# Latent attention on one Trainium2 core: joining the two halves of a head's output by a vector add instead of a shift matmul

## The chip, the cores and the metric

The kernel runs on one core of a Trainium2 chip. The metric is the device time in microseconds of one execution, as the median of several runs. TensorE does the matmuls and the transposes into PSUM; VectorE, ScalarE and GpSimd do the element-wise work, and only the first two of these touch PSUM here; SyncE, ScalarE and GpSimd issue DMAs.

## What is computed

Two decoder layers over 1024 positions of width 1024. Each projects the residual stream once; the columns feed a gated linear recurrence (8 heads), a latent attention (8 heads) and an attention into 256 memory tokens (4 heads). Each group's output is gated, the groups are concatenated, projected back and normalised. The change touches the latent attention alone, whose core is

```
for l in range(DEPTH):
    ...
    y_mla = _mla_group(...)          # 8 heads, 64 value columns each
    ...
    y = concatenate([y_hg * silu(hg_gate), y_mla * silu(mla_gate), y_mem * silu(mem_gate)])
    x = layernorm(ALPHA * x + y @ w_out[l])

# inside _mla_group, per block of 128 queries
s = (einsum('bqhd,bkhd->bhqk', qn, k_nope) + einsum('bqhr,bkr->bhqk', qr, k_rope)) * scale
p = softmax(where(key_idx <= q_idx, s, NEG_BIG))
o = einsum('bhqk,bkhd->bqhd', p, v)
```

All data are f32. To keep the precision, the kernel writes each operand of a product as the sum of a rounded part and a remainder (`split`, L288) and forms the product from three matmuls (`mm3`, L262).

## The kernel before, in words

A layer runs through its stages one after another: memory attention, the latents, the recurrence, the latent attention (`mla_prep`, L913, and `mla_attend`, L965), the output product (`out_group`, L1155). The latent attention takes about 736 to 892 us in the first layer and 1806 to 1978 us in the second.

`mla_attend` walks over 32 steps: 8 heads `hd`, and for each four pairs `j` of query blocks, 256 queries. A pair of query blocks sees 2j + 2 blocks of 128 keys, so the pairs grow from j = 0 to j = 3. For a step:

- `scores` (L992) forms the score matrix of two query blocks in PSUM (tile `A`, two buffers), adds the causal mask by a matmul with the identity (L1014), takes the negated row maximum `nm` on VectorE (L1017), the exponential `pr` with its row sum `rs` on ScalarE (L1020), the reciprocal on VectorE (L1021) and the scaling on GpSimd (L1024). It is called one step ahead.
- `turn` (L1029) transposes the probabilities of a pair of key blocks on TensorE (L1034) and splits them into `ph` on ScalarE (L289) and the remainder `pl` on VectorE (L290).
- `values` (L1042) multiplies them with the values. The weight tile `VV` holds a head's 64 value columns twice: the rounded part in columns 0 to 63, the remainder in 64 to 127. So one matmul with `ph` (L1058) and one with `pl` (L1059) write a sum of 128 rows into a PSUM tile `B` of 256 columns, whose lower 64 rows (0 to 63) hold one half of the result and whose rows 64 to 127 hold the other. These units are queued, and one is taken when more than three wait.
- After the last unit of a step, ScalarE copies the 128 rows into `ol` (L1062). One unit later `close` (L1065) multiplies this copy by a constant matrix `shift` (L1069), which moves rows 64 to 127 onto rows 0 to 63 and adds them to the sum in PSUM. VectorE then multiplies rows 0 to 63 by the head's gate (L1072), and a DMA writes the result `yt` to `Yd` in DRAM (L1073).

An even head's result lies in partitions 0 to 63 of `yt`, an odd head's in 64 to 127 (`rw`). Between the steps come the query products of the next head (`q_proj`, L971, with L985 on ScalarE and L986 on VectorE), for every second head its keys (`k_proj`, `k_odd`, L943 and L956), and in the last head the first weight and input tiles of the output product (L1136, L1145). The source gives the order of the calls; a scheduler sets the order of the instructions on each engine, and each engine runs its queue in that order.

The matrix is made once at the start: GpSimd clears it (L157) and ScalarE copies 64 columns of the identity into it (L158).

Of the kernel before, what the change touches and what calls it, by code (L numbers as in the profile page):

```python
# [7 lines left out]
F32 = mybir.dt.float32  # L8
F32R = mybir.dt.float32r
# [3 lines left out]
ALU = mybir.AluOpType  # L13
# [4 lines left out]
P = 128  # L18
# [23 lines left out]
C_ID = 0  # L42
# [39 lines left out]
def program(tc, xT, xtok, memT, pos, w_in, small, w_uq, w_uk, w_uv, w_mk, w_mv,  # L82
            w_out, ln_g, ln_b, cst, msk, out):
    nc = tc.nc
    es = ExitStack()

    def pool(name, **kw):
        return tc.tile_pool(name=name, **kw)

    cp = es.enter_context(pool("cp", bufs=1))  # L90
# [26 lines left out]
    def T(pl, shape, dt=F32, tag=None, bufs=None):  # L117
        n_name[0] += 1
        return pl.tile(shape, dt, tag=tag, name=f"{tag}_{n_name[0]}", bufs=bufs)
# [7 lines left out]
    def f32(t):  # L127
        return t.bitcast(F32)
# [8 lines left out]
    NSM = small.shape[1]  # L137
    sm = T(cp, [P, NSM], F32, "sm")

    shift = T(cp, [P, P], F32R, "shift")  # L140
    mhalf = T(cp, [P, 8], F32, "mhalf")
    nc.gpsimd.memset(mhalf, -0.5)
    ones = T(cp, [P, 2], F32, "ones")
# [9 lines left out]
    def constants(lp):  # L153
        cs = T(wpc[1], [P, 2048], F32, "raw", 2)[:, 0:C_N]
        nc.scalar.dma_start(cs, cst)
        nc.scalar.dma_start(sm, small)
        nc.gpsimd.memset(f32(shift), 0.0)  # L157
        nc.scalar.copy(shift[:, 0:64], cs[:, C_ID + 64:C_ID + P])  # L158
        nc.scalar.copy(idr, cs[:, C_ID:C_ID + P])
        for i, c in enumerate((C_BE, C_BO)):  # L160
            nc.scalar.copy(bias_r[i], cs[:, c:c + P])
# [803 lines left out]
    def mla_attend(l, cqT, ckT, KK, uq, kv, k_proj, k_odd, rtab, VV, lp, rp):  # L965
        uqh, uql = (t.rearrange("p (r c) -> p r c", r=2) for t in uq)
        gs = []
# [72 lines left out]
        opss = {}  # L1040

        def values(hd, j, cp_, ph, pl_):  # L1042
            hp, ab = hd // 2, hd % 2
            rw = slice(64 * ab, 64 * ab + 64)
            if cp_ == 0:
                opss[hd, j] = psB()
            ops = opss[hd, j][:, 0:256].rearrange("p (b q) -> p b q", b=2)
# [10 lines left out]
                nc.tensor.matmul(ov, lhsT=w, rhs=rh, start=kb_ == 0, stop=False)  # L1058
                nc.tensor.matmul(ov, lhsT=w, rhs=rl, start=False, stop=kb_ == 2 * j + 1)  # L1059
            if cp_ == j:  # L1060
                t = T(lp, [P, 256], F32R, "ol", 1)
                nc.scalar.copy(t, opss[hd, j][:, 0:256])  # L1062
                return t

        def close(hd, j, t):  # L1065
            hp, ab = hd // 2, hd % 2
            rw = slice(64 * ab, 64 * ab + 64)
            ops = opss.pop((hd, j))
            nc.tensor.matmul(ops[:, 0:256], lhsT=shift, rhs=t, start=False, stop=True, skip_group_check=True)  # L1069
            s_ = slice(j * 256, (j + 1) * 256)  # L1070
            yt = T(lp, [P, 256], F32, "yt", 2)
            nc.vector.tensor_tensor(out=yt[rw], in0=ops[0:64, 0:256], in1=gs[hp][rw, s_], op=ALU.mult)  # L1072
            (nc.gpsimd if hd == 7 and j > 1 else nc.sync).dma_start(Y[8 + hp, rw, s_], yt[rw])  # L1073

        def v_proj(tb):
# [49 lines left out]
        if ends:  # L1125
            close(*ends.pop())
# [201 lines left out]
    for l in range(DEPTH):  # L1328
# [4 lines left out]
        ops = latents_out(l, X, tp)  # L1333
# [75 lines left out]
```

## Time and profile before

| | |
|---|---|
| median of 3 runs | 2161.31 us (2160.71 to 2161.49) |
| profiled execution, its own time | 2163.67 us |
| its span, from first to last instruction | 2161.9 us |
| mean granted TensorE clock | 0.986 |
| first and last shift matmul | 736.6 and 1977.8 us |

The views of the profile used here are these. The page's first part gives for each engine its busy time, the share of the span and the number of instructions. A table by windows gives the same for stretches of time, with the granted clock and the DMA load. A view by line gives the duration of a line's instructions, what its engine waited for before them and who waited for them. A time line lists single instructions: start, duration, engine, line, operation, tiles written and read, and in brackets the engine's idle time ahead of it with what ended it. The chain of waits goes back from the last instruction of the program, at each step to what released it. PE is TensorE's matmul, PEld its weight load, DVE VectorE, ACT ScalarE, POOL GpSimd, SP SyncE.

### The profile page before, as it was taken

How to read it: one execution, taken by the hardware profiler on the slowest of the kernel's cores; microseconds unless marked ns; L12 is line 12 of the kernel's file. 1: busy time of each engine (PE TensorE's matmuls, PEld its weight loads, DVE VectorE, ACT ScalarE, POOL GpSimd, SP SyncE). 2: the span in 40 equal slices, each digit the busy share in tenths (PEclk: the TensorE clock that was granted, in tenths of full speed). 3: DMA queues.
4: the chain of work that ended last, by engine and by line, in shares of the span. 5: the costliest groups of instructions: out<-in, count | busy, mean ns of one | idle time of the engine just before them, and what ended most of it. 6: DMA issues, size and time to landing. Idle time of an engine off the chain costs nothing. (4 is left out here: it accounts for less than half of the span.)

```text
span 2161.9 us, 30334 instructions
## 1 busy us (share of the span) xinstructions
PE 2065.4 (96%) x11176; PEld 1752.7 (81%) x11176; DVE 1459.8 (68%) x2665; ACT 1009.8 (47%) x1999; POOL 375.3 (17%) x516
## 2 busy tenths in 40 slices
PE   9997999999999899999899989999999997999998
PEld 7887888888887788788687878888888886888886
DVE  6536777777777788566764366777777776887524
ACT  5534343434343677444554444434443436775311
POOL 0212000000001445211111220000000014543112
PEclk9999999999999999999999989999999999999999
DMA  5413101111114301456761131111111134015322
GB/s 199 132 59 127 52 27 59 40 59 40 59 40 162 116 15 38 152 188 229 234 194 47 59 130 41 40 59 39 59 40 50 49 131 146 13 40 180 109 66 78
DMA packets 122100, 194.47 MB, mean 90 GB/s; under 512 B 8608, under 2 KB 90400, under 8 KB 121952
## 3 DMA queue, kind: packets, MB, share of 16 engines
q1 hardware_dynamic: 100560, 145.91, 20.8%
q10 hardware_dynamic: 13840, 22.24, 3.1%
q0 software_dynamic: 7552, 24.39, 3.0%
q8 instruction: 88, 1.44, 0.3%
q14 instruction: 60, 0.49, 0.1%
HBM read 151.09 MB, written 41.42 MB: 89 GB/s over the span
## 5 line engine op out<-in xcount | busy, mean ns | idle before, releaser
L263 PE MATMUL Y<-x,wh 128*128 128x512 f32 x576 | 233.9, 406 | 0.0
L265 PE MATMUL Y<-x,wl 128*128 128x512 f32 x576 | 232.4, 404 | 0.0
L264 PE MATMUL Y<-x,wh 128*128 128x512 f32 x576 | 228.3, 396 | 0.0
L249 DVE TENSOR_TENSOR wl<-raw,wh 128x512 fp32r<-128x512 f32 (+2 forms) x216 | 141.3, 701 | 102.0 <-ACT wh L248 81.9
L264 PE MATMUL Y<-t,wh 128*128 128x512 f32 x432 | 170.9, 396 | 0.0
L263 PE MATMUL Y<-t,wh 128*128 128x512 f32 x432 | 169.9, 393 | 0.0
L265 PE MATMUL Y<-t,wl 128*128 128x512 f32 x432 | 168.9, 391 | 0.0
L289 ACT CAST wh<-raw 128x512 fp32r<-128x512 f32 (+1 forms) x124 | 72.9, 592 | 199.8 <-DMA raw<-in_w_in 132.5
L248 ACT CAST wh<-raw 128x512 fp32r<-128x512 f32 (+2 forms) x216 | 118.7, 605 | 98.4 <-PE A L264 49.8
L289 ACT CAST wh<-S 128x512 fp32r<-128x512 f32 x144 | 89.5, 622 | 138.2 <-DVE S L687 61.6
L573 PEld LDWEIGHTS B<-Q,r 128*128 128x128 f32 x896 | 115.5, 191 | 38.8 <-issue 13.5
L1024 POOL TENSOR_SCALAR pr<-pr,rs 128x512 f32<-128x512 f32 (+1 forms) x192 | 116.8, 617 | 147.9 <-DVE rs L1021 132.6
L573 PE MATMUL B<-Q,r 128*128 128x128 f32 x896 | 132.2, 291 | 7.9 <-DVE Q L552 7.8
L290 DVE TENSOR_TENSOR pl<-B,ph 128x512 fp32r<-128x512 f32 (+1 forms) x192 | 119.9, 644 | 22.4 <-ACT ph L289 19.0
L290 DVE TENSOR_TENSOR wl<-raw,wh 128x512 fp32r<-128x512 f32 (+1 forms) x124 | 80.8, 655 | 80.2 <-ACT wh L289 79.8
L265 PEld LDWEIGHTS Y<-x,wl 128*128 128x128 f32 x576 | 109.2, 190 | 20.4
L263 PEld LDWEIGHTS Y<-x,wh 128*128 128x128 f32 x576 | 109.6, 190 | 19.2
L264 PEld LDWEIGHTS Y<-x,wh 128*128 128x128 f32 x576 | 109.3, 190 | 19.4
L1020 ACT ACTIVATE pr<-A,nm 128x128 f32<-128x128 f32 (+7 forms) x128 | 95.5, 747 | 57.8 <-DVE nm L1017 54.3
L289 ACT CAST ph<-B 128x512 fp32r<-128x512 f32 (+1 forms) x192 | 102.7, 554 | 36.3 <-PE B L1034 20.4
L285 POOL TENSOR_TENSOR rst<-ss,mhalf 128x4 f32<-128x4 f32 x32 | 36.4, 1137 | 474.1 <-DVE ss L283 455.7
L263 PE MATMUL A<-wh,yh 128*128 128x512 f32 x288 | 112.7, 396 | 5.6 <-ACT wh L248 3.6
(337 smaller groups left out, 5583.6 us busy)
## 6 DMA issues: line engine op xcount, KB each, us to landing
raw<-in_w_in SPq DMA_DIRECT2D x84, 512.0 KB, 4.6
raw<-in_w_out SPq DMA_DIRECT2D x32, 1024.0 KB, 5.4
yr<-Yd SPq DMA_DIRECT2D x28, 384.0 KB, 4.8
Yd<-r POOLq DMA_DIRECT2D x32, 256.0 KB, 2.6
raw<-in_w_mk SPq DMA_DIRECT2D x8, 512.0 KB, 4.8
raw<-in_w_mv SPq DMA_DIRECT2D x8, 512.0 KB, 4.4
t<-in_xT SPq DMA_DIRECT2D x16, 256.0 KB, 3.2
Yd<-yt POOLq DMA_DIRECT2D x16, 256.0 KB, 2.3
```

The lines of the kernel that those rows point to most:

```text
L248: nc.scalar.copy(h[:, s_], raw[:, s_])
L249: nc.vector.tensor_tensor(out=lo[:, s_], in0=raw[:, s_], in1=f32(h[:, s_]), op=ALU.subtract)
L263: nc.tensor.matmul(o, lhsT=lh, rhs=rh, start=first, stop=False, **kw)
L264: nc.tensor.matmul(o, lhsT=lh, rhs=rl, start=False, stop=False, **kw)
L265: nc.tensor.matmul(o, lhsT=ll, rhs=rh, start=False, stop=last, **kw)
L285: nc.gpsimd.tensor_tensor(out=r[:, 0:k], in0=ss, in1=mhalf[:, 0:k], op=ALU.pow)
L289: nc.scalar.copy(h, src)
L290: nc.vector.tensor_tensor(out=lo, in0=src, in1=f32(h), op=ALU.subtract)
L573: nc.tensor.matmul(lp[:, pr * P:(pr + 1) * P], lhsT=xp[:, pr * P:(pr + 1) * P], rhs=q_moving(Q, pr, b), start=True, stop=True)
L1020: nc.scalar.activation(po, sv, AF.Exp, bias=nm, scale=1.0, accum_out=rs)
L1024: nc.gpsimd.tensor_scalar(out=pr[:, c0:c1], in0=pr[:, c0:c1], scalar1=rs, scalar2=0.0, op0=ALU.mult, op1=ALU.add)
```

## The change

The shift matrix and the shift matmul go. ScalarE copies only rows 64 to 127 of the sum, now as plain f32 into one of two buffers; VectorE adds this copy to rows 0 to 63 and writes `yt`, and a second vector instruction multiplies `yt` by the gate in place.

```diff
-    shift = T(cp, [P, P], F32R, "shift")
...
-        nc.gpsimd.memset(f32(shift), 0.0)
-        nc.scalar.copy(shift[:, 0:64], cs[:, C_ID + 64:C_ID + P])
...
             if cp_ == j:
-                t = T(lp, [P, 256], F32R, "ol", 1)
-                nc.scalar.copy(t, opss[hd, j][:, 0:256])
+                t = T(lp, [P, 256], F32, "ol", 2)
+                nc.scalar.copy(t[64:128], opss[hd, j][64:128, 0:256])
                 return t
 
         def close(hd, j, t):
...
             ops = opss.pop((hd, j))
-            nc.tensor.matmul(ops[:, 0:256], lhsT=shift, rhs=t, start=False, stop=True, skip_group_check=True)
             s_ = slice(j * 256, (j + 1) * 256)
             yt = T(lp, [P, 256], F32, "yt", 2)
-            nc.vector.tensor_tensor(out=yt[rw], in0=ops[0:64, 0:256], in1=gs[hp][rw, s_], op=ALU.mult)
+            nc.vector.tensor_tensor(out=yt[rw], in0=ops[0:64, 0:256], in1=t[64:128], op=ALU.add)
+            nc.vector.tensor_tensor(out=yt[rw], in0=yt[rw], in1=gs[hp][rw, s_], op=ALU.mult)
```

Three lines fewer ahead of them, lines after L158 carry numbers lower by 3 in the changed kernel; there the add is L1068 and the gate product L1069. The scheduler also arranges the neighbours anew. On VectorE, in the second layer, where head 0 and head 1 close: before (`yt` with the gate `mg` is the gate product, `pl` a remainder, `nm` a row maximum, `rs` a reciprocal),

```order
L290 TENSOR_TENSOR pl_16732<-B_16726,ph_16731 128x512
L1021 RECIPROCAL rs_16720<-rs_16720 128x1
L1072 TENSOR_TENSOR yt_16741<-B_16679,mg_16128 64x256
L290 TENSOR_TENSOR pl_16750<-B_16744,ph_16749 128x512
L290 TENSOR_TENSOR pl_16763<-B_16757,ph_16762 128x512
L290 TENSOR_TENSOR pl_16777<-B_16772,ph_16776 128x384
L1072 TENSOR_TENSOR yt_16786<-B_16735,mg_16128 64x256
L1017 TENSOR_REDUCE nm_16794<-A_16789 128x1
L1017 TENSOR_REDUCE nm_16806<-A_16801 128x1
```

and with the change:

```order
L287 TENSOR_TENSOR pl_16729<-B_16723,ph_16728 128x512
L1018 RECIPROCAL rs_16717<-rs_16717 128x1
L1068 TENSOR_TENSOR yt_16737<-B_16676,ol_16697 64x256
L287 TENSOR_TENSOR pl_16747<-B_16741,ph_16746 128x512
L1069 TENSOR_TENSOR yt_16737<-yt_16737,mg_16125 64x256
L287 TENSOR_TENSOR pl_16760<-B_16754,ph_16759 128x512
L287 TENSOR_TENSOR pl_16774<-B_16769,ph_16773 128x384
L1068 TENSOR_TENSOR yt_16782<-B_16732,ol_16767 64x256
L1014 TENSOR_REDUCE nm_16791<-A_16786 128x1
L1069 TENSOR_TENSOR yt_16782<-yt_16782,mg_16125 64x256
L1014 TENSOR_REDUCE nm_16803<-A_16798 128x1
```

Each product has become two instructions, with another one between them; the second maximum stands behind one instruction more.

On VectorE a little earlier, ahead of the query products `qf` of the next head: before,

```order
L290 TENSOR_TENSOR pl_16568<-B_16563,ph_16567 128x384
L986 TENSOR_TENSOR qf_16586<-B_16579,rtab_16050 64x512
L986 TENSOR_TENSOR qf_16598<-B_16591,rtab_16050 64x512
L290 TENSOR_TENSOR K_3131_16047<-B_16604,K_3130_16046 64x512
L290 TENSOR_TENSOR K_3131_16047<-B_16611,K_3130_16046 64x512
```

and with the change:

```order
L287 TENSOR_TENSOR pl_16565<-B_16560,ph_16564 128x384
L1068 TENSOR_TENSOR yt_16663<-B_16470,ol_16572 64x256
L1069 TENSOR_TENSOR yt_16663<-yt_16663,mg_16125 64x256
L983 TENSOR_TENSOR qf_16583<-B_16576,rtab_16047 64x512
L983 TENSOR_TENSOR qf_16595<-B_16588,rtab_16047 64x512
```

Head 0's last close, which stood behind the keys and the maxima (L1072 with `yt_16667`, eight rows after `qf`), now stands ahead of `qf`. In each layer six closes stand so.

On TensorE, ahead of the scores of head 2 that wait for the exponential (tile `A`, 320 columns): before,

```order
L1034 MATMUL B_16813<-idr_64,pr_16710 128x128
L1034 MATMUL B_16813<-idr_64,pr_16722 128x128 x2
L1058 MATMUL B_16780<-ph_16749,VV_16039 128x256
L1059 MATMUL B_16780<-pl_16750,VV_16039 128x256
L1058 MATMUL B_16780<-ph_16749,VV_16039 128x256
L1059 MATMUL B_16780<-pl_16750,VV_16039 128x256
L263 MATMUL A_16827<-K_3130_16046,qh_16577 128x320
```

and with the change:

```order
L1031 MATMUL B_16810<-idr_64,pr_16719 128x128 x2
L1055 MATMUL B_16777<-ph_16746,VV_16036 128x256
L1056 MATMUL B_16777<-pl_16747,VV_16036 128x256
L1055 MATMUL B_16777<-ph_16746,VV_16036 128x256
L1056 MATMUL B_16777<-pl_16747,VV_16036 128x256
L1055 MATMUL B_16777<-ph_16759,VV_16036 128x256
L1056 MATMUL B_16777<-pl_16760,VV_16036 128x256
L1055 MATMUL B_16777<-ph_16759,VV_16036 128x256
L1056 MATMUL B_16777<-pl_16760,VV_16036 128x256
L1055 MATMUL B_16777<-ph_16773,VV_16036 128x256
L1056 MATMUL B_16777<-pl_16774,VV_16036 128x256
L260 MATMUL A_16824<-K_3129_16043,qh_16574 128x320
```

Six value matmuls that came after these scores now come ahead of them; it is so at heads 2 and 4 of both layers. On SyncE's queue, in the last head, the first weight load of the output product (L1136) moves ahead of three stores of `yt` and of the first load from `Yd` (L1145); the second one moves behind one more store.

## Rows read from the trace of the kernel before

**Rows 1.** The page's first part: busy time, share of span, instructions.

```profile
PE 2065.4 (96%) x11176; PEld 1752.7 (81%) x11176; DVE 1459.8 (68%) x2665; ACT 1009.8 (47%) x1999; POOL 375.3 (17%) x516
```

**Rows 2.** Table by windows, the two attention stages: length, then busy time per engine.

```profile
736.00:890.00 154.00, 148.74 (x1006) 134.47 (x1004) 127.60 (x252) 112.68 (x259) 79.04 (x113) 1.00 0.11 32
1806.00:1977.00 171.00, 165.09 (x1099) 148.78 (x1099) 141.58 (x275) 123.10 (x281) 86.53 (x124) 1.00 0.11 31
```

**Rows 3.** Chain of waits, 1841 to 1854 us: start, duration, what.

```profile
1845.77 0.70 POOL pr L1024
...
1850.90 0.55 issue
1851.45 0.42 DVE yt L1072
...
1851.90 0.57 DVE nm L1017
...
1853.03 0.20 ACT pr L1020
```

**Rows 4.** Time line of TensorE, the scores at 1853 us.

```profile
1853.28 0.42 PE L263 MATMUL A<-K,qh 128*128 128x320 f32 x1 [0.16 <-ACT pr L1020]
```

**Rows 5.** Table by windows, 1841 to 1853 and 1853 to 1863 us.

```profile
1841.00:1853.00 12.00, 11.25 (x85) 10.13 (x83) 10.87 (x22) 8.91 (x20) 4.03 (x7) 1.00 0.08 18
1853.00:1863.00 10.00, 9.84 (x60) 8.87 (x59) 6.67 (x14) 5.79 (x15) 6.08 (x10) 1.00 0.03 7
```

**Rows 6.** Time line of TensorE, two shift matmuls, and the matmul behind one.

```profile
1845.55 0.39 PE L1069 MATMUL B<-ol,shift 128*128 128x256 f32 x1 [0.47 <-ACT ol L1062]
...
1890.21 0.28 PE L1069 MATMUL B<-ol,shift 128*128 128x256 f32 x1
1890.33 0.60 PE L1034 MATMUL B<-idr,pr 128*128 128x128 f32 x4
```

**Rows 7.** By line: the shift matmul; who waited for the copy L1062.

```profile
L1069 PE MATMUL B<-ol,shift x64: 277/331/389, 736.6 to 1977.8; 128*128 128x256 f32 x64
...
  PEld B L1069: 8.3, 20
  PE B L1069: 3.8, 12
```

**Rows 8.** Durations: gate product; vector instruction from SBUF; copies of 64 and 128 partitions.

```profile
L1072 DVE TENSOR_TENSOR yt<-B,mg x64: 403/417/419, 737.0 to 1978.2; 64x256 f32<-64x256 f32 x64
...
L290 DVE TENSOR_TENSOR wl<-raw,wh 128x256 fp32r<-128x256 f32 x16 | 6.2, 420 | 0.3 <-ACT wh L289 0.3
...
L953 ACT COPY kb<-B 64x512 f32<-64x512 f32 x6 | 3.5, 581 | 0.4
...
L289 ACT CAST ph<-B 128x512 fp32r<-128x512 f32 x47 | 27.3, 585 | 3.7 <-PE B L1034 3.4
```

**Rows 9.** By line: the copy into the shift matrix and its wait.

```profile
L158 ACT CAST shift<-raw x1: 244/244/244, 24.9 to 24.9; 128x64 fp32r<-128x64 f32 x1
...
  DMA raw<-in_cst: 3.0, 1
```

**Rows 10.** Time line of VectorE, gate products of heads 0 and 1.

```profile
1842.97 0.69 DVE L290 TENSOR_TENSOR pl<-B,ph 128x512 fp32r<-128x512 f32 x1
1843.58 0.41 DVE L1072 TENSOR_TENSOR yt<-B,mg 64x256 f32<-64x256 f32 x1
...
1848.86 0.42 DVE L1072 TENSOR_TENSOR yt<-B,mg 64x256 f32<-64x256 f32 x1
1849.31 0.69 DVE L290 TENSOR_TENSOR pl<-B,ph 128x512 fp32r<-128x512 f32 x1
```

**Rows 11.** By line and shape, 736 to 890 us: query products on VectorE.

```profile
L986 DVE TENSOR_TENSOR qf<-B,rtab 64x512 f32<-64x512 f32 x12 | 8.2, 687 | 7.7 <-ACT qf L985 7.7
```

**Rows 12.** Time line: SyncE's second weight load, and TensorE's wait at the output product.

```profile
872.23 0.37 SPq L1136 DMA_DIRECT2D raw<-in_w_out  x1
...
909.91 0.50 PE L263 MATMUL A<-wh,yh 128*128 128x512 f32 x1 [2.00 <-ACT yh L289]
```

## The prediction

> **What bounds the kernel now.** I read the engine totals first, then the two attention stages alone, then the shift matmul with its neighbours, then the chain of waits in one stretch of attention. TensorE is busy 96% of the span, and no other engine passes 68% [rows 1]. The change lives in two stages, 736 to 890 us and 1806 to 1977 us. There TensorE is busy 313.8 of 325.0 us, but VectorE is busy 269.2 of 325.0 as well [rows 2], 83% instead of its 68% average. So the stage has one engine in front and a second close behind, and the change moves work from the first to the second.
>
> The chain of waits shows that they change places within one pair of heads, which takes a quarter of the second stage, some 42 us [rows 2]. For most of a pair the chain is matmul after matmul. From 1845.8 to 1853.2 it goes through GpSimd, then ScalarE, a vector product of this very line (0.42), the row maximum (0.57) and the exponential, and only then to a matmul [rows 3]; that matmul, the first of the next scores, had indeed been kept waiting, by 0.16 us [rows 4]. VectorE is busy 10.87 of 12.00 us from 1841 to 1853, but only 6.67 of 10.00 in the ten after it [rows 5]. Its slack is real, and unevenly spread.
>
> **What is removed.** 64 shift matmuls, 32 in each layer. One that waits for nothing takes the array's place for 0.12 us: it starts at 1890.21, the next matmul at 1890.33 [rows 6]. That is 64 x 0.12 = 7.7 us. A shift matmul also needs the copy on ScalarE, made only after the last product, and TensorE stood idle for that 12 times, 3.8 us in all; 20 further waits, 8.3 us, are put down to its weight load [rows 7], which partly overlaps earlier matmuls. The one at 1845.55 stood idle 0.47 us [rows 6]. If everything passes through, TensorE saves at least 7.7 + 3.8 = 11.5 us, at most 7.7 + 3.8 + 8.3 = 19.8. I take 11.5, since a weight load that waits behind a running matmul costs nothing.
>
> The copy on ScalarE stays. It now takes 64 partitions of 256 columns, not 128. For 512 columns, a copy of 64 partitions takes 581 ns and one of 128 partitions 585 [rows 8], so half the partitions save nothing. Its second buffer takes away a wait for the reader of the buffer, which was not among the waits seen: nothing. Both edits of the start-up cost nothing: the copy into the shift matrix came after 3.0 us of waiting for a DMA on ScalarE [rows 9], and TensorE does not read the matrix before 736.6 us [rows 7]; were that cover gone, it is 0.24 us.
>
> **What is added.** 64 vector instructions: the one product of each close becomes an add (PSUM and the copy) and a gate product (SBUF alone). The add has the form of today's product, 417 ns; the gate product's nearest row, 256 columns from SBUF, takes 420 [rows 8]. What one of them takes from the queue depends on its neighbour. The product of head 0 at 1843.58 starts 0.08 us before the vector instruction ahead of it ends (1842.97 + 0.69); that of head 1 at 1848.86 is followed only 0.03 us after its end, at 1849.31 [rows 10]. So a step costs 0.33 us where it overlaps and 0.45 where it doesn't. Between these, the added work is 64 x 0.33 = 21 us, or up to 64 x (0.45 + 0.12) = 36 us where its follower is held up too. Head 1 writes the upper 64 partitions, head 0 the lower; that is what differs between them. The add always reads its copy from the upper 64 while its neighbours read from the lowest, so I expect it to behave like head 1's. Even heads then go from 0.33 to two unoverlapped steps, 0.90; odd ones from 0.57 (0.45, and 0.12 on the follower) to 1.02. The mean addition is 0.51 us, 33 us in all, against 325.0 - 269.2 = 56 us in which VectorE idles.
>
> The Trainium skill (VectorE: DVE Perf Modes, section "Two Vector instructions with no wait between them") says that a vector instruction whose operands or output begin in another group of 32 partitions than those of the last access to that memory waits until all earlier ones have finished. By that rule, the trace agrees for heads 0 and 1, the added work is the 33 us of the last paragraph; without it the new steps would overlap, the work be 21 us, the dense stretch not late, and rival 2 below fall away.
>
> **Where the added work falls.** The order shows that part of it goes into idle time: in 12 of the closes, the pair now stands just ahead of the query products, where VectorE waits 0.64 us each time for ScalarE (7.7 us over 12) [rows 11]. Three closes of each pair of heads stay in the dense stretch. They bring 3 x 0.51 = 1.5 us to 12.00 - 10.87 = 1.13 us of idle time, so the maxima there come about 0.4 us late. The order of the matmuls has an answer: at heads 2 and 4 of both layers six value matmuls of the same 256 columns, 6 x 0.12 = 0.72 us, now stand ahead of the scores that wait for this exponential. So I count no new loss there, but no gain either: the stretch ends when VectorE lets it, and what TensorE saves inside is not collected. Inside are three of a pair's eight shift matmuls and the 0.47 us idle: 3 x 0.12 + 0.47 = 0.83.
>
> **The sum.** 11.5 / 8 = 1.44 us per pair of heads (four in each layer), less 0.83, is 0.61; times 8 that is 4.9. The profiled execution took 2163.67 us, its span 2161.9 and 1.8 around it; it becomes 2158.8. It lies 2.4 us over the median of the runs, 2161.31, so against that I predict 2156.4. Other moves cost nothing by themselves: on SyncE's queue a weight load for the output product moves ahead of three small stores; those loads come long before their use, the later of the two issued at 872.23, while TensorE first stands still for the output product at 909.91, for 2.00 us [rows 12]. That cover gone, it would be of the order of those 2 us a layer. The bank of the sum is freed by the add, not the product, so no later than now.
>
> **Rivals.** (1) TensorE is the bound throughout, and everything passes: 2161.3 - 11.5 = 2149.8, with all of the weight-load waits 2141.5. For it speaks the 96%; against it that the chain leaves TensorE in every pair. (2) VectorE becomes the bound in the dense stretch: its gaps there are waits for ScalarE that move along when everything is late, and so take up nothing. Each pair then loses 3 x 0.51 = 1.5 us, 8 x 1.5 = 12, less the 4.9 saved elsewhere: 2161.3 + 7.3 = 2168.6, or 2173 with nothing saved. It decides once the maxima at the end of the stretch come more than the 0.72 us of moved matmuls late; at 0.33 a step (1.0 us, under the 1.13 idle) it could not happen. For it speaks that VectorE would have 269 + 33 = 302 us of work in 325; against it, the moved steps. (3) The change does nothing that counts: the freed places are spent waiting for the probabilities or their remainders, as at 1853.28 [rows 4]: 2161.3.
>
> **How the numbers follow.** A measurement here tells about 0.2%, 4.3 us, from no change. Chances: the forecast 0.50 (its own range 2152 to 2161, three fifths of it below 2157.0, the rest within 0.2%), everything passes 0.17, VectorE bound 0.20, nothing 0.13. Faster: 0.30 + 0.17 = 0.47; slower 0.20; the same 0.20 + 0.13 = 0.33. The range 2147 to 2169 leaves out the ends of the first two rivals.
>
> **What would show it.** In the profile after: 64 matmuls fewer; two vector lines of 64 at about 415 to 420 ns; VectorE busy some 290 to 300 us over the two stages; the attention stages shorter by 2 to 3 us each, and everything behind them unchanged. The row of waits of the scores for the exponential must not grow by more than a few microseconds. I am wrong if those waits, or value matmuls waiting for the remainders, grow by more than 7 us (then rival 2), or if the stages shrink by 6 us or more each (rival 1).

## The result and the profile after

| | before | after |
|---|---|---|
| median of 4 runs each | 2161.40 us (2160.71 to 2162.48) | 2177.01 us (2174.55 to 2179.41) |
| profiled execution, and its span | 2163.67, 2161.9 us | 2174.55, 2172.8 us |
| mean granted TensorE clock | 0.986 | 0.985 |
| attention stage, layers 0 and 1 | 156.4, 156.4 us | 161.7, 162.7 us |
| between the two stages | 929.1 us | 927.8 us |
| behind the second | 184.9 us | 184.5 us |

The change makes the kernel slower by 0.7%: the ratio of the times is 1.0072, with a 95% interval of 1.0054 to 1.0089. An attention stage is counted here from the start of its first value matmul to that of its last. The two stages together grew by 11.6 us, the start of the first came 1.1 us later, and nothing else grew. That accounts for the 10.9 us between the two profiled executions. Between the medians lie 15.6 us; the profiled execution after was the fastest of its four, and where the others spent the rest was not seen.

The page's first part, after, to be set beside [rows 1]: TensorE has its 64 matmuls fewer and VectorE its 64 instructions more.

```profile
PE 2063.1 (95%) x11112; PEld 1744.2 (80%) x11112; DVE 1488.7 (69%) x2729; ACT 1017.5 (47%) x1998; POOL 370.2 (17%) x515
```

The table by windows, each window one attention stage: before, over the stages just defined (so not the edges of [rows 2]). Behind the length stand the busy times of PE, PEld, DVE, ACT and POOL, then the granted clock, the DMA share and GB/s.

```profile
735.00:891.40 156.40, 151.14 (x1026) 136.88 (x1025) 129.91 (x254) 113.98 (x261) 79.96 (x114) 1.00 0.11 32
1820.60:1977.00 156.40, 151.23 (x1028) 137.09 (x1025) 129.91 (x254) 113.93 (x261) 79.90 (x114) 1.00 0.12 34
```

The same table after.

```profile
736.10:897.70 161.60, 150.38 (x996) 133.19 (x995) 143.76 (x285) 117.77 (x261) 78.76 (x114) 1.00 0.11 31
1825.50:1988.20 162.70, 151.61 (x996) 134.82 (x995) 143.81 (x285) 117.98 (x261) 78.97 (x114) 0.99 0.11 32
```

Three things stand here. VectorE's busy time grew by 13.9 us a stage. ScalarE's grew by 3.9 us, with the same number of instructions and a copy of half the rows. And TensorE's did not fall, although 32 matmuls a stage are gone. A matmul's busy time is not the place that it takes: the shift matmuls, all of one size, are recorded with 277 to 389 ns [rows 7], while the next matmul can start 0.12 us after one [rows 6]. So the 96% of [rows 1] was no proof that TensorE set the pace.

The 0.99 in the second row after has a place. For 3.4 us of the second stage TensorE was granted half its clock, 1.2 instead of 2.4 GHz:

```profile
1958.20:1964.20 6.00, 3.76 (x29) 3.23 (x28) 5.86 (x10) 4.89 (x10) 4.60 (x5) 1.00 0.22 67
1964.20:1967.60 3.40, 3.40 (x19) 3.40 (x18) 2.85 (x10) 2.52 (x8) 0.72 (x2) 0.50 0.11 24
```

Head 6, in which this stretch lies, took 22.5 us there and 21.4 in the first stage, which has none; the other heads agree between the stages to 0.1 us. So 1.1 of the 11.6 us go with the lower clock. In the 6 us before it TensorE was busy for 3.76. At the same place of the first stage it was busy for 3.74 of 6 us and the clock did not fall, so what decides this stays open.

By line and tile, after: the two vector instructions of a close, and the copy. They take what [rows 8] let one expect.

```profile
L1068 DVE TENSOR_TENSOR yt<-B,ol x64: 416/417/419, 738.1 to 1989.0; 64x256 f32<-64x256 f32 x64
L1069 DVE TENSOR_TENSOR yt<-yt,mg x64: 397/422/496, 738.6 to 1989.4; 64x256 f32<-64x256 f32 x64
L1059 ACT COPY ol<-B x64: 367/367/369, 737.4 to 1988.6; 64x256 f32<-64x256 f32 x64
```

The time line of VectorE after, in the dense stretch that [rows 3] showed before.

```profile
1851.27 0.42 DVE L1068 TENSOR_TENSOR yt<-B,ol 64x256 f32<-64x256 f32 x1
...
1852.77 0.42 DVE L1069 TENSOR_TENSOR yt<-yt,mg 64x256 f32<-64x256 f32 x1
...
1855.06 0.42 DVE L1068 TENSOR_TENSOR yt<-B,ol 64x256 f32<-64x256 f32 x1
...
1856.23 0.42 DVE L1069 TENSOR_TENSOR yt<-yt,mg 64x256 f32<-64x256 f32 x1
1856.68 1.16 DVE L287 TENSOR_TENSOR pl<-B,ph 128x512 fp32r<-128x512 f32 x2
1857.87 0.42 DVE L1068 TENSOR_TENSOR yt<-B,ol 64x256 f32<-64x256 f32 x1
1858.32 0.56 DVE L1014 TENSOR_REDUCE nm<-A 128x1 f32<-128x384 f32 x1
1858.91 0.42 DVE L1069 TENSOR_TENSOR yt<-yt,mg 64x256 f32<-64x256 f32 x1
```

No row between 1851.27 and 1860.65 has an idle time in brackets: for 9.4 us each instruction of VectorE starts within 0.1 us of the end of the one ahead, and six of its instructions, 2.5 us, are those of closes. The chain of waits after goes along them, from the last maximum through the exponential to the scores:

```profile
1859.36 0.70 DVE nm L1014
...
1860.98 0.44 PE A L260
```

Before, the chain in this place held one product and lasted as long as [rows 3] show. Last, the waits of TensorE in the first stage (total us, times, longest), before:

```profile
PE A L263 <- ACT pr L1020: 1.5, 4, 1.0
PEld B L1034 <- DVE pl L290: 0.5, 2, 0.3
```

and after. The scores wait twice as long for the exponential. The transposes behind earlier value products, which hardly waited for VectorE's remainder `pl`, now stand for it (before, a matmul L1034 had no row of this kind, only its weight load).

```profile
PEld B L1031 <- DVE pl L287: 5.1, 8, 1.7
...
PE B L1031 <- DVE pl L287: 3.6, 8, 1.6
...
PE A L260 <- ACT pr L1017: 3.1, 9, 0.7
```

Where in a stage the loss lies can be read from the end of the last copy of each head, in the time line of ScalarE. Heads 1, 3 and 5, which hold the dense stretches, took 22.7, 22.7 and 24.1 us before and 23.7, 23.6 and 25.4 after (layer 0). Head 7 went from 11.1 to 12.9, head 0 (from its first copy) from 13.7 to 14.3; heads 2, 4 and 6 changed by 0.3 or less.

### The profile page after: what moved, and what is told of

Same layout as the page of the kernel before. It is cut to its first block, busy times and chain, and to the rows that moved or that the text cites. A ratio compares the mean times of both kernels' runs of the same rounds, so it can differ in the third digit from the quotient of the medians.

```text
span 2172.8 us, 30139 instructions
## 1 busy us (share of the span) xinstructions
PE 2063.1 (95%) x11112; PEld 1744.2 (80%) x11112; DVE 1488.7 (69%) x2729; ACT 1017.5 (47%) x1998; POOL 370.2 (17%) x515
## 4 chain that ended last, share of the span: by engine, by line
PE 61%; DVE 15%; issue 7%; ACT 5%; DMA 5%; POOL 2%; ACTq 0%; POOLq 0%; SPq 0%; DVEq 0%
PE Y L260 7%; PE Y L261 7%; PE Y L262 7%; PE A L260 6%; PE A L262 6%; PE A L261 6%; PE B L570 5%; PE B L260 3%; PE B L262 3%; PE B L261 3%; DMA raw<-in_w_in 3%; DVE pl L287 2%; ACT pr L1017 2%; DVE wl L287 2%; DVE nm L1014 2%
## 5 line engine op out<-in xcount | busy, mean ns | idle before, releaser
L1021 POOL TENSOR_SCALAR pr<-pr,rs 128x512 f32<-128x512 f32 (+1 forms) x192 | 116.2, 615 | 161.1 <-DVE rs L1018 144.9
L287 DVE TENSOR_TENSOR yl<-yr,yh 128x768 fp32r<-128x768 f32 (+1 forms) x44 | 43.2, 989 | 109.1 <-ACT yh L286 107.3
```

The lines of the kernel that those rows point to most:

```text
L287: nc.vector.tensor_tensor(out=lo, in0=src, in1=f32(h), op=ALU.subtract)
L1021: nc.gpsimd.tensor_scalar(out=pr[:, c0:c1], in0=pr[:, c0:c1], scalar1=rs, scalar2=0.0, op0=ALU.mult, op1=ALU.add)
```

## The experiments

Each run is compared with runs of the kernel before on its own chip. The stage lengths come from the profiled execution. The three kernels with the order and the time of before (itself, e9, e11) lie within 156.0 and 156.5 us. A star in the table stands for 3.4 us of the stage at 1.2 GHz; the rest of the stages ran at 2.4. Where neither stage of a kernel has a star, the two agree to 0.5 us. Where only one has, it is the longer one, by 0.7 to 1.5 us, in e14 by 2.4. So stages without a star can be compared to about 0.5 us, and those with one to 1 us or more. The stretch between the stages varied from 922 to 931 us without regard to the edit.

The order of the instructions is a second thing that differs, since the scheduler makes it anew for each kernel. Leaving out the edited lines, TensorE, VectorE and ScalarE have one order in before, e9, e10 and e11; a second in the change, e3, e6, e7 and e12; a third in e1, e2, e4, e5 and e8. e13, e14 and e15 have one each of their own. Only within such a group does a comparison leave the order out.

| run | time against before, 95% interval | stages, us |
|---|---|---|
| the change | 1.0072 [1.0054, 1.0089] | 161.7, 162.7* |
| e1 before, no shift matmul | 1.0015 [1.0005, 1.0024] | 157.0, 157.0 |
| e2 change, no gate product | 1.0038 [1.0024, 1.0052] | 161.2**, 160.1** |
| e3 change, copy to rows 0 to 63 | 1.0043 [1.0028, 1.0057] | 161.2*, 160.3 |
| e4 change, gate product on GpSimd | 1.0042 [1.0027, 1.0057] | 159.6, 161.1** |
| e5 e1 with the half copy | 1.0026 [1.0015, 1.0037] | 159.5**, 159.6* |
| e6 change, full copy | 1.0053 [1.0034, 1.0073] | 160.8, 160.5 |
| e7 change, lower half copied | 1.0060 [1.0040, 1.0080] | 161.8*, 160.7 |
| e8 e6 with gate product on GpSimd | 1.0027 [1.0016, 1.0037] | 158.4, 159.1* |
| e9 before, shift matmul of 64 columns | 0.9999 [0.9989, 1.0009] | 156.0, 156.4 |
| e10 before, all products held | 1.0015 [1.0005, 1.0026] | 157.3, 157.1 |
| e11 before, halves swapped for odd heads | 1.0001 [0.9991, 1.0010] | 156.5, 156.4 |
| e12 e1 with a second product | 1.0045 [1.0029, 1.0060] | 160.9*, 160.5* |
| e13 e1 without the product | 0.9991 [0.9981, 1.0000] | 153.1, 153.1 |
| e14 before, sum copied by ScalarE | 1.0115 [1.0097, 1.0133] | 164.9, 167.3* |
| e15 change, gate product of 32 columns | 1.0066 [1.0046, 1.0087] | 161.0, 161.3 |

**e1, the removal alone.**

```diff
-            nc.tensor.matmul(ops[:, 0:256], lhsT=shift, rhs=t, start=False, stop=True, skip_group_check=True)
```

> The kernel before without its shift matmul; the copy on ScalarE and the one gate product per close stay. It leaves out the lower half of each head's output. It tells what the 64 matmuls and their waits are worth when VectorE has nothing more to do. Theory Q (VectorE's queue is what costs: the matmuls are worth something, the added vector instructions more): the step priced at 4.9 to 11.5 us comes out, 2150 to 2157 us. Rival O (the new order of the neighbours costs, not VectorE's time: the scheduler's order here is also another than before): no gain or a loss, 2161 us or more.

The stages did not get shorter, as rival O had it. TensorE is busy 3.3 us less in each (151.2 before) and stands idle 9.1 us instead of 5.2:

```profile
735.20:892.20 157.00, 147.86 (x997) 133.24 (x995) 130.44 (x254) 113.03 (x261) 78.90 (x115) 1.00 0.11 32
```

The order here is not that of before, so e9 asked again with that one.

**e9, the shift matmul at a quarter of its columns, all orders unchanged.**

```diff
-            nc.tensor.matmul(ops[:, 0:256], lhsT=shift, rhs=t, start=False, stop=True, skip_group_check=True)
+            nc.tensor.matmul(ops[:, 0:64], lhsT=shift, rhs=t[:, 0:64], start=False, stop=True, skip_group_check=True)
```

> The kernel before with the shift matmul cut from 256 to 64 columns; every engine's order stays as before. Left out: the lower rows of three quarters of the output. Theory C (TensorE is not short of time where the shift matmul stood, it only arrives earlier at waits for the chain of exponential, GpSimd scaling and ph and pl): stages 156 to 157 us, time 0.999 to 1.001. The forecast's step (TensorE's time is what the stage is made of): three quarters of 0.107 us by 64 is 5 us, stages 153.5 to 154.5, time 0.9975 to 0.998.

No change in the time or in the stages. The matmul itself had become shorter:

```profile
L1069 PE MATMUL B<-ol,shift x64: 191/244/299, 735.7 to 1970.0; 128*128 128x64 f32 x64
```

So three quarters of the shift matmul's columns were worth nothing, with no help from a different order. The matmul's waits for its copy remain in e9; only e1 takes them away as well, and gains nothing either, in another order.

**e2 to e4, parts of the added work.**

```diff
 # e2
-            nc.vector.tensor_tensor(out=yt[rw], in0=yt[rw], in1=gs[hp][rw, s_], op=ALU.mult)
 # e3
-                nc.scalar.copy(t[64:128], opss[hd, j][64:128, 0:256])
+                nc.scalar.copy(t[0:64], opss[hd, j][64:128, 0:256])
-            nc.vector.tensor_tensor(out=yt[rw], in0=ops[0:64, 0:256], in1=t[64:128], op=ALU.add)
+            nc.vector.tensor_tensor(out=yt[rw], in0=ops[0:64, 0:256], in1=t[0:64], op=ALU.add)
 # e4
-            nc.vector.tensor_tensor(out=yt[rw], in0=yt[rw], in1=gs[hp][rw, s_], op=ALU.mult)
+            nc.gpsimd.tensor_tensor(out=yt[rw], in0=yt[rw], in1=gs[hp][rw, s_], op=ALU.mult)
```

> The changed kernel without the gate product: one vector instruction per close, as before, but it is the add that reads the copy from partitions 64 to 127. The gate of the latent attention is left out of the result. Theory Q: within 5 us of the kernel before without its shift matmul, the difference being the price of steps that don't overlap (some 0.1 to 0.2 us in 32 closes): 2152 to 2160 us. Rival O: it stays above 2170, since the matmuls are ordered anew here too.

> The changed kernel with the copy written to partitions 0 to 63 of its tile, so that the add of an even head has all its operands there; the order of the instructions on TensorE and VectorE is that of the changed kernel. Theory Q with the rule on overlapping steps: the even heads' 32 closes save up to 2 x 0.12 us each, 7.7 us of VectorE's time in all; with VectorE the bound, 3 to 8 us less than the changed kernel, 2169 to 2174. If steps that don't overlap don't matter: 2176 to 2178. Rival O: unchanged, as the order is unchanged.

> The changed kernel with the gate product on GpSimd, which is busy half of the attention stage. VectorE again has one instruction per close. Theory Q: 2150 to 2162 us, as without the gate product or up to 5 us more, if GpSimd's scaling of the probabilities comes late behind the products (64 of them at an estimated 0.5 to 0.7 us, from its 128x256 scaling of 0.57 us). Rival O: above 2170.

By the mean of its two stages each took 1.4 to 1.9 us back, and none took back most. e3's ratio lies where theory Q had it. e2 and e4 took longer than Q allowed, near the lower edge of rival O. But O does not explain them: they have e1's order, and as many vector instructions as e1, and are still 2.6 us longer than its 157.0 in e4's first stage, which has no star. So neither the number of vector instructions nor the order is all of it. What these three have in common with the change and not with e1 is ScalarE's copy from partition 64 on. Around it the time line of ScalarE shows a difference. Before:

```profile
1845.05 0.19 ACT L1020 ACTIVATION_READ_ACCUMULATOR pr<-A,nm 128x1 f32 x1
1845.14 0.36 ACT L1062 CAST ol<-B 128x256 fp32r<-128x256 f32 x1
1845.39 0.98 ACT L289 CAST ph<-B 128x512 fp32r<-128x512 f32 x2
```

After:

```profile
1850.65 0.19 ACT L1017 ACTIVATION_READ_ACCUMULATOR pr<-A,nm 128x1 f32 x1
1850.87 0.37 ACT L1059 COPY ol<-B 64x256 f32<-64x256 f32 x1
1851.26 0.97 ACT L286 CAST ph<-B 128x512 fp32r<-128x512 f32 x2
```

The copy of 128 rows starts 0.10 us before its predecessor ends (1845.05 + 0.19) and its follower 0.11 us before it ends. The copy of 64 rows starts 0.03 us after one end and is followed 0.02 us after its own. Of 64 copies, 61 started before their predecessor's end before the change and none after it. Where a copy stands close between two others this takes up to 0.27 us of ScalarE's time; by its busy time the mean is 3.9 us over 32 closes, 0.12 us each.

**e5 to e8, the copy and the vector instructions apart.** e5 is e1 with the half copy; e6 to e8 start from the change.

```diff
 # e5, in e1
-                nc.scalar.copy(t, opss[hd, j][:, 0:256])
+                nc.scalar.copy(t[64:128], opss[hd, j][64:128, 0:256])
 # e6, and e8 with e4's line
-                nc.scalar.copy(t[64:128], opss[hd, j][64:128, 0:256])
+                nc.scalar.copy(t, opss[hd, j][:, 0:256])
 # e7
-                nc.scalar.copy(t[64:128], opss[hd, j][64:128, 0:256])
+                nc.scalar.copy(t[0:64], opss[hd, j][0:64, 0:256])
...
-            nc.vector.tensor_tensor(out=yt[rw], in0=ops[0:64, 0:256], in1=t[64:128], op=ALU.add)
+            nc.vector.tensor_tensor(out=yt[rw], in0=ops[64:128, 0:256], in1=t[0:64], op=ALU.add)
```

> The kernel before without the shift matmul, as in the first run, and the ScalarE copy cut to rows 64 to 127; VectorE has no instruction more than before. Left out: the sum of the halves. Theory A (ScalarE: an instruction that begins at partition 64 no longer overlaps its two neighbours, about 0.27 us per copy, 32 copies a layer): attention stages of 160 to 162 us against 157.0 in the first run, time 1.003 to 1.005 of before; the copy starts after its predecessor's end on ScalarE. Theory B (VectorE: the added instruction, or its operands' partitions): stages stay at 157, time 1.001 to 1.002.

> The changed kernel with the copy over all 128 rows, as before the change; the add still reads rows 64 to 127 of it. Theory A: ScalarE overlaps again, stages of 156.5 to 159 us against 161.7 and 162.7 of the change, time 0.999 to 1.003. Theory B: VectorE is unchanged, stages stay at 161 to 163, time 1.004 to 1.008.

> The changed kernel with rows 0 to 63 copied and the add reading rows 64 to 127 from PSUM: 64 partitions as in the change, but beginning at partition 0. Theory A, where the partition of the beginning decides: ScalarE overlaps, stages of 156.5 to 159 us, time 0.999 to 1.003. Theory A2, where the half number of partitions decides: no overlap, 161 to 163, 1.004 to 1.008. Theory B: 161 to 163, and ScalarE's overlap makes no difference.

> The changed kernel with the full copy and the gate product on GpSimd, so that VectorE has as many instructions as before. Theory A: 155 to 157.5 us a stage, time 0.997 to 1.001. Theory B: as with the gate product alone on GpSimd, 159.6 to 161.1 a stage, 1.003 to 1.005.

Neither theory held alone. e5 bears out the ScalarE part, though it stays under theory A's range: with not one vector instruction more, and in e1's order, the half copy lengthens the stages from 157.0 to 159.5 us, and ScalarE's busy time goes up by 5 us. Its stages have stars; up to the end of head 4, before the first of these stretches, e5 is 0.9 us behind e1.

```profile
735.90:895.40 159.50, 150.25 (x997) 136.22 (x996) 130.85 (x254) 118.15 (x261) 79.17 (x115) 0.98 0.11 32
```

But e6, where ScalarE overlaps again, falls only to 160.65 us (mean of its stages), missing the 156.5 to 159 that theory A gave. In the first stages, which have no star, that is 0.9 us less than the change. The intervals of the two times overlap, so this price rests on the stage lengths:

```profile
736.20:897.00 160.80, 150.18 (x997) 133.10 (x996) 143.97 (x285) 114.24 (x261) 78.85 (x114) 1.00 0.11 31
```

The orders are the change's there, so the 3.65 us between e1 and e6 belong to the added vector instruction, with its start held back by the partitions of its operands (its hold), its wait for the copy and the order that comes with it. e7 tells what it is about the half copy. Its copy has 64 rows as well, but begins at partition 0, and overlaps:

```profile
1848.32 0.19 ACT L1017 ACTIVATION_READ_ACCUMULATOR pr<-A,nm 128x1 f32 x1
1848.42 0.35 ACT L1059 COPY ol<-B 64x256 f32<-64x256 f32 x1
1848.67 0.95 ACT L286 CAST ph<-B 128x512 fp32r<-128x512 f32 x2
```

The copy of e3, which reads from row 64 and writes from row 0, doesn't:

```profile
1841.79 0.19 ACT L1017 ACTIVATION_READ_ACCUMULATOR pr<-A,nm 128x1 f32 x1
1842.01 0.37 ACT L1059 COPY ol<-B 64x256 f32<-64x256 f32 x1
1842.40 0.97 ACT L286 CAST ph<-B 128x512 fp32r<-128x512 f32 x2
```

So the partition of the beginning decides, not the number of rows. And it is the difference from the neighbour that counts: in six closes of the change the follower is `qf` of an odd head (L982), which reads and writes from partition 64 on like the copy. In all six it overlaps the copy, by 0.10 us:

```profile
775.36 0.37 ACT L1059 COPY ol<-B 64x256 f32<-64x256 f32 x1
775.63 0.59 ACT L982 ACTIVATE qf<-B 64x512 f32<-64x512 f32 x1
```

e7's second stage, without a star like e6's, is as long as that one (160.7 and 160.5); the time that theory A gave it was missed for the same reason. e8 has VectorE's number of instructions of before and a free ScalarE, and comes within 2.4 us a stage, between its two expectations. In the first stages, with one order and no stars, e4 is 1.2 us above e8, which again prices the half copy, and e8 1.4 us above e1, which prices the add's hold and wait and GpSimd's product together.

**e10 and e11, the hold on VectorE.** The gate product of before doesn't overlap its neighbours for odd heads [rows 10]. e10 makes it so for all heads, e11 was meant to free all, both in the order of before.

```diff
 # e10
-            nc.vector.tensor_tensor(out=yt[rw], in0=ops[0:64, 0:256], in1=gs[hp][rw, s_], op=ALU.mult)
+            nc.vector.tensor_tensor(out=yt[64:128], in0=ops[0:64, 0:256], in1=gs[hp][64:128, s_], op=ALU.mult)
...
 # e11
-        nc.gpsimd.memset(f32(shift), 0.0)
...
+        nc.scalar.copy(shift[:, 64:P], cs[:, C_ID:C_ID + 64])
...
-            nc.vector.tensor_tensor(out=yt[rw], in0=ops[0:64, 0:256], in1=gs[hp][rw, s_], op=ALU.mult)
+            nc.vector.tensor_tensor(out=yt[rw], in0=ops[rw, 0:256], in1=gs[hp][rw, s_], op=ALU.mult)
...
-            split(VV[:, tb, :, 0:64], VV[:, tb, :, 64:128], acc.rearrange("p (h v) -> p h v", h=8))
+            v = VV[:, tb]
+            vh, vl = (bass.AP(tensor=v.tensor, offset=v.offset + o,
+                              ap=[list(v.ap[0]), [2 * P, 4], [st, 2], [1, 64]]) for o, st in ((0, 192), (64, 64)))
+            split(vh, vl, acc.rearrange("p (a b v) -> p a b v", a=4, b=2))
```

> The kernel before, order unchanged, with every gate product writing rows 64 to 127 from sums in rows 0 to 63, where before only the odd heads' did; the even heads take the odd heads' gate. No instruction is added. Theory D (the hold of VectorE is a price of its own, about 0.23 us for each of 16 more products a layer, part of it on the path): stages 157.5 to 160, time 1.001 to 1.003. Rival (only added instructions cost): stages 156 to 157, time 0.999 to 1.001.

> The kernel before, TensorE's order unchanged, with the high and low halves of V swapped for odd heads and a shift matrix that swaps the halves, so that odd heads' sums stand in rows 64 to 127 and no gate product crosses partitions. Theory D: VectorE regains its overlap at 32 products, stages 153 to 155.5 us, time 0.997 to 0.9995. Rival: stages 156 to 157, time 0.999 to 1.001.

In e10, 16 more held products a stage cost 0.8 us, about 0.05 us each: a price, but under the range of stages that was expected for it. e11 missed, because its premise failed. A product that reads and writes partitions 64 to 127 throughout is still not overlapped; here it is between neighbours that begin at partition 0:

```profile
1843.45 1.22 DVE L290 TENSOR_TENSOR pl<-B,ph 128x512 fp32r<-128x512 f32 x2 [0.20 <-ACT ph L289]
1844.70 0.43 DVE L1072 TENSOR_TENSOR yt<-B,mg 64x256 f32<-64x256 f32 x1
1845.16 1.16 DVE L1017 TENSOR_REDUCE nm<-A 128x1 f32<-128x384 f32 x2
```

So it is not enough that one instruction stays in its partitions; where its neighbours begin counts.

**e12 and e13, the number of vector instructions.** Both start from e1.

```diff
 # e12
             nc.vector.tensor_tensor(out=yt[rw], in0=ops[0:64, 0:256], in1=gs[hp][rw, s_], op=ALU.mult)
+            nc.vector.tensor_tensor(out=yt[rw], in0=yt[rw], in1=gs[hp][rw, s_], op=ALU.mult)
 # e13
...
-            nc.vector.tensor_tensor(out=yt[rw], in0=ops[0:64, 0:256], in1=gs[hp][rw, s_], op=ALU.mult)
-            (nc.gpsimd if hd == 7 and j > 1 else nc.sync).dma_start(Y[8 + hp, rw, s_], yt[rw])
+            (nc.gpsimd if hd == 7 and j > 1 else nc.sync).dma_start(Y[8 + hp, rw, s_], t[0:64])
```

> The kernel before without the shift matmul, as in the first run, with a second gate product in place behind the first: one more VectorE instruction for each close, as in the change, the full copy, and no instruction whose operands newly lie in other partitions than its output. Left out: the sum of the halves; the gate is put on twice. Theory E (the added instruction itself is the larger part of VectorE's price): stages 159 to 160.5 us against 157.0, time 1.003 to 1.005. Rival (the held operands of the add are): stages 157 to 158, time 1.001 to 1.0025.

> The kernel before without the shift matmul and without the gate product: the copy of rows 0 to 63 goes out as it is, so VectorE has one instruction fewer per close than before and two fewer than the change. Left out: the sum of the halves and the gate. Theory E (each VectorE instruction of a close lengthens a stage, as one more did by 3.7 us): stages 153 to 155 us against 157.0 of the first run, time 0.995 to 0.998. Rival (VectorE has room up to the number it had before, and is short only beyond it): stages 156 to 157.5, time 0.999 to 1.001.

With none, one and two vector instructions per close the stages take 153.1, 157.0 and 160.7 us; e13's and e12's first stages:

```profile
733.90:887.00 153.10, 144.78 (x995) 132.29 (x993) 118.63 (x223) 113.22 (x261) 79.58 (x115) 1.00 0.11 33
```

```profile
733.70:894.60 160.90, 151.12 (x998) 134.52 (x995) 142.74 (x285) 114.30 (x261) 79.00 (x114) 0.99 0.10 31
```

The step down is 3.9 us and the step up 3.7. Both of e12's stages have a star, and its head 6 is 0.9 us longer than that of e6, which has none; without that the step up is an estimated 2.8 us. So each of 32 instructions of 0.42 us is worth 0.09 to 0.12 us of the stage. Head 1 takes 21.6, 22.6 and 23.6 us, and head 7 10.6, 11.6 and 12.7 (last copy to last copy).

e12 has the change's order and not e1's, so how much of the step up is the order's is not shown. For the step down the order is nearly left out in head 1: but for the four products, VectorE and ScalarE have the same order in e1 and e13, and on TensorE one pair of value matmuls moved; the head takes 1.0 us less. e13 also hands the sum's PSUM buffer back after the copy and not after the product, but in e1 TensorE's matmuls waited for that product only 1.2 us, over both stages. So VectorE had no slack in this dense stretch even before: what it was relieved of there shows.

e12 and e6 share their order and differ in what the second instruction reads. Heads 1, 3 and 5 take the same in both (23.6, 23.6 and 25.2 us in the first stage). So the add's hold and its wait for the copy cost nothing in the dense stretches; in the other heads they cost some 0.9 us a stage, once e12's stretch at the lower clock is taken off. Of e13's 6.6 us in the stages only about 2 us appeared in the time; where the others went isn't settled.

**e14, a version without the vector instruction.**

```diff
-            nc.vector.tensor_tensor(out=yt[rw], in0=ops[0:64, 0:256], in1=gs[hp][rw, s_], op=ALU.mult)
+            nc.scalar.copy(yt[rw], ops[0:64, 0:256])
+            nc.gpsimd.tensor_tensor(out=yt[rw], in0=yt[rw], in1=gs[hp][rw, s_], op=ALU.mult)
```

> The kernel before with the shift matmul kept, its sum copied out by ScalarE and the gate product on GpSimd: VectorE one instruction fewer per close than before, ScalarE and GpSimd one more each. Theory E, with ScalarE's copies at 0.37 us overlapped and GpSimd idle half the stage: 154 to 157 us, time 0.996 to 1.000; a version that beats both. Rival (ScalarE and GpSimd stand in the same chain of exponential, scaling and ph, and an added instruction costs there what it costs on VectorE): 158 to 161 us, time 1.002 to 1.005.

This is the slowest of all, beyond its rival's figure. TensorE's transposes and GpSimd now wait for the copy on ScalarE:

```profile
POOL yt L1073 <- ACT yt L1072: 17.2, 14, 2.3
...
PE B L1034 <- ACT yt L1072: 7.0, 10, 2.6
...
ACT yt L1072 <- DMA Yd<-yt: 6.9, 7, 2.6
```

The last row adds that ScalarE itself stood for the output buffer, whose write now comes after a 0.76 us product on GpSimd. ScalarE was busy 73% of the stage before, less than VectorE, and still had no room for this copy in that place.

**e15, a shorter second instruction.**

```diff
-            nc.vector.tensor_tensor(out=yt[rw], in0=yt[rw], in1=gs[hp][rw, s_], op=ALU.mult)
+            nc.vector.tensor_tensor(out=yt[rw, 0:32], in0=yt[rw, 0:32], in1=gs[hp][rw, j * 256:j * 256 + 32], op=ALU.mult)
```

> The changed kernel with the gate product over 32 of 256 columns, so the instructions stay in number and VectorE's time falls by about 0.23 us per close, 7.5 us a layer. Left out: the gate of the other columns. Theory E1 (VectorE's time is what counts): stages 160 to 161 us against 162.2, time 1.003 to 1.005. E2 (the number of instructions and the waits between them): 161.5 to 163, time 1.005 to 1.008. In all of them the order that the scheduler makes differs a little, so a shift under 0.7 us tells nothing.

The instruction fell from 422 to 192 ns and the stages to 161.15 us, between the two expectations; the time points to E2. Against the change's first stage, heads 1 and 3 took 0.5 us less and head 7 1.2 us less, which speaks for E1 there. Heads 2, 4, 5 and 6 together, most of all 5 and 6, where the order differs most, took 1.9 us more. So the run as a whole doesn't tell the two apart.

No version tried beats the kernel before. e13, which leaves both the sum and the gate out, is 0.1% faster with an interval that ends at 1.0000, so by this interval a version that moved them into a later stage could gain 0.2% at the most. It was not tried.

## Why the prediction was wrong

It said 2156.4 us, in a range of 2147 to 2169; the result is 2177.0. By its own steps:

- **What bounds the kernel.** That VectorE and TensorE change places within a pair of heads was right. That TensorE is in front for the rest, by its 96%, was not shown: e9 takes three quarters of the shift matmuls' columns away, some 0.36 us a head by the prediction's price, and heads 2, 4 and 6 of the first stage take 0.1 us less at most. At the lower clock head 6 did get longer, so TensorE is not off the path there either.
- **What is removed.** The 64 matmuls went, but the 11.5 us did not come. e9 takes away three quarters of the 7.7 us of places and gains nothing. e1 takes away all, with the waits for the copy, and its two stages are 1.2 us longer, in another order; TensorE's idle time there grew from 5.2 to 9.1 us a stage.
- **The copy, "half the partitions save nothing", priced at zero.** The duration was right (378 ns before, 367 after). The step looked at the duration alone and not at the neighbours, although the next paragraph did just that for VectorE. ScalarE behaves alike: the copy that begins at partition 64 lost its overlap on both sides. By the runs this is 0.9 us a stage (e6 to the change) or 1.2 (e8 to e4), each in first stages of one order without a stretch at the lower clock; from e1 to e5 it is 2.5, with such stretches in e5. The Trainium skill (ScalarE: Activation LUTs, section "What ACT_TABLE_LOAD costs") states that back-to-back ACTIVATE instructions overlap by about 93 ns. The copies of before, which the trace calls CAST, agree with a median of 110 ns, and the trace after shows when that is lost.
- **What is added.** Rightly sized. VectorE's busy time grew by 287.6 - 259.8 = 27.8 us over both stages, where 33 were forecast within 21 to 36, and the add of even heads overlapped its predecessor in none of 32 closes, as expected. Of the even heads' gate products, expected not to overlap either, 16 of 32 did. That hold itself is a minor price (e10).
- **Where the added work falls: the step that failed.** It set 1.5 us of work against 1.13 us of idle time in the dense stretch, let the rest be covered by the six value matmuls moved ahead of the scores, and so counted no loss there. The idle times were not slack but VectorE's waits within the same chain. e13 shows it: with one vector instruction fewer per close, head 1 is 1.0 us and a stage 3.9 us shorter than e1's, though e1's VectorE, busy 130.4 of 157.0 us, had idle time already. With one more, a stage is 3.65 us longer (e6) or an estimated 2.8 (e12), in another order. After the change VectorE runs 9.4 us almost without a gap, and heads 1 and 3 take about 1 us and head 5 1.4 us longer in spite of the moved matmuls. Outside the dense stretch, head 7, behind which no query products follow, lost 1.8 us that the step did not count.
- **The sum.** In place of 4.9 us saved the two stages grew by 11.6. For the first stage, which has no stretch at the lower clock in any of these, that can be walked through in single steps: 156.4 (before), 157.0 without the matmul (e1), 160.8 with the add as a second vector instruction (e6), 161.7 with the half copy (the change). The first two steps change the order as well. The second stage adds 1.1 us with the lower clock.
- **The rivals.** It went as rival (2), VectorE the bound in the dense stretch, which had 0.20. It named the mechanism ("waits for ScalarE that move along when everything is late"), and its 12 us with nothing saved elsewhere is close to the 11.6 of the stages. That is in part luck: ScalarE's share and 1.1 us at the lower clock are in the 11.6, and heads 0 and 7 lost time as well as the dense stretches. Its upper end, 2173, was left out of the range, which ended at 2169; either way the result lies above.
- **Everything behind unchanged** was right: 929.1 and 927.8 us between the stages, 184.9 and 184.5 behind.
- **What would show it.** The matmuls and durations came as written, VectorE's 290 to 300 us nearly (287.6). The waits warned in part. Over both stages the scores' waits for the exponential grew by 3.1 us at the matmuls (3.4 to 6.5), under the 7 that were named, but by 8.4 at their weight loads (3.4 to 11.8), over it, as rival 2 had it. The value matmuls' waits for the remainders grew by 1.1. The transposes' waits for `pl`, which were not named, grew from nothing to 7.2 us at the matmuls.

## What to carry to other kernels

An engine's idle time inside a chain of dependent instructions is not room for more work: see what its gaps wait for, and if that is the chain itself, price an added instruction as late from the first one on. Busy TensorE time is no measure of what fewer matmuls give back: shorten one in place, with the order unchanged, before counting on it. When variants differ by 1 us a stage, compare the order of their instructions and the granted clock of the stage before putting the difference down to the edit. And where an instruction is cut to some partitions, look at where it begins as well as at how long it takes, since both of its neighbours may lose their overlap with it.

## What was not expected of the hardware

On ScalarE too an instruction that begins at another partition than its neighbours runs alone: its start moved from 0.11 us before the end of its predecessor to 0.02 us after it, and its follower's likewise, with 64 rows read from partition 64 (the change, e3, e5), but not with 64 rows from partition 0 (e7), nor towards a follower that begins at 64 too (six closes of the change). On VectorE the same holds for an instruction that lies in partitions 64 to 127 in all its operands (e11): moving everything to the same upper half frees nothing as long as the neighbours begin at 0. And TensorE's clock fell to 1.2 GHz for 3.4 us in some stages and not in others of the same kernel; in five of the six kernels with such stretches in one stage alone, that stage was 0.7 to 1.5 us longer than the other.
